# The first stage's squares added up before TensorE, wider idle products, and weight splits further ahead

## The chip, the core and the metric

The kernel runs on one core of a Trainium2 chip. A core has five engines with queues of their own: TensorE (PE in the rows; its weight loads are listed apart as PEld), VectorE (DVE), ScalarE (ACT), GpSimd (POOL) and SyncE (SP, which here issues the DMA transfers). Each engine takes its instructions in the order in which the program lists them and waits on semaphores for what it needs. The metric is the device time of one execution, in microseconds (us).

## What is computed

The reference runs two transformer blocks on 256 tokens of 1024 features in float32. Only the beginning of the first block matters here:

```python
def rms_norm(x, g):
    xf = x.astype(jnp.float32)
    y = xf * lax.rsqrt(jnp.mean(xf * xf, axis=-1, keepdims=True) + EPS)
    return (y * g.astype(jnp.float32)).astype(x.dtype)
...
silu_c, silu_cc = jax.nn.silu(c), jax.nn.silu(c_ctx)
mod_x = (silu_c @ w_ada + b_ada)[:, None, :]
mod_c = silu_cc @ w_ada + b_ada
px = modulate(rms_norm(x, g_pre_mix), sh_m, sc_m) @ w_in
pc = modulate(rms_norm(ctx, g_pre_mix), csh_m, csc_m) @ w_in
```

Here x and ctx are 256 x 1024 each and w_in projects to attention and mLSTM inputs. After that come windowed attention, a gated recurrent memory (mLSTM), an output projection and a feed-forward layer, and then a second block of the same size.

## The kernel before

**Layout.** Tokens lie along the free axis and features along the 128 partitions: x is the tile `X` (inside `XT`), ctx is `CT`, each 8 feature tiles (k = 0 to 7) of 256 tokens. Every weight product is made of three in a reduced-precision float type: `prep_item` (line 377) takes the next piece of weights from the buffer `raw`, ScalarE copies its high part to `H` (line 384), VectorE subtracts to get the low part `L` (line 385), and `mm3` (lines 430 to 432) multiplies H with the high part of x, H with the low part and L with the high part.

**The list of pieces.** A planner fixes one list of pieces in the order of use. Most are weight pieces of up to eight 128-column blocks. Between them stand 1024-wide rows of the modulation matrix ("ada" pieces below), for which `prep_item` issues one VectorE reduction (line 391) instead of a split. Raw pieces are loaded by SyncE into six buffers, a new load when a buffer is read out (line 374). `block` (line 412) hands out the next block; when it takes a new piece it first prepares pieces until `la` + 1 are ready, so `la` is how many pieces are split ahead of the one in use. There are four buffers each for H and L. The first stage uses eight weight pieces, w0 to w7, one for each k; the next ones are M0, M1, M2 (the run `mkak`, 24 blocks), V0, V1, V2 (the run `v1`, 8 blocks in pieces of 3, 3 and 2), then one piece for each step of `MIX1` (q2, o0, ...). With w2 to w5, and with each of M0 to V2, goes one ada piece behind the weight piece.

**`start`, the first stage.** The inputs are loaded, `awake` issues idle products of a tile of ones (line 629) as the loads arrive, and the squares of x and ctx are made in four halves of 4 feature tiles x 256 tokens (three by ScalarE, line 642, one by VectorE, line 640). TensorE sums them over the features: for each half 8 products with one output column (line 645). The sums go through a square root (line 693) and five small VectorE steps to a diagonal matrix (line 533). `mod_rows(k)` (line 661) computes the shift and scale of feature tile k from an `araw` tile of 1 MB, `mod_cols` and `mod_of` put them into columns. A 512-column product (line 706) spreads the roots over the partitions as `psb`. `inp(k)` makes the normalised, modulated input of tile k in high and low parts (VectorE line 683, ScalarE line 684, VectorE line 687). Then a loop over k runs `mod_rows(k + 1)` and 24 products of the tile (12 of 336 columns, 12 of 256), and in its middle prepares the next weight piece and `inp(k + 1)`.

**`mix1`.** It copies the stage's results out, rotates two query tiles (`rope`), and runs `mkak` and `v1` while `ml_gates`, `conv` and `ml_ctx` advance step by step in hooks between the blocks. All of these are on VectorE and ScalarE in the order in which the program lists them. `ml_ctx` makes `kw` on VectorE from a transposed key tile, and TensorE then multiplies it (line 983).

Of the kernel before, what the change touches and what calls it, by code (L numbers as in the profile page):

```python
# [13 lines left out]
AF = mybir.ActivationFunctionType  # L14
ALU = mybir.AluOpType
# [4 lines left out]
KD = 8  # L20
SEQ = 256
# [7 lines left out]
MIX1 = (  # L29
    "A c c c q2 c a0 A o0 a1 b0 A a2 A b1 A a3 b2 q3 b3 A t o1 A t t t t t o2 A m t A t k o3 A s"  # L30
)
WAKE = (14, 4, 4, 4, 4)
ADA0 = (0, 0, 1, 1, 1, 1, 0, 0)
ADA1 = (1, 1, 1, 1, 1, 1, 1, 1, 1, 1, 1, 1)
BACK = 8
# [279 lines left out]
class Builder:  # L315
# [112 lines left out]
    def mm3(self, out, H, L, xh, xl, start, stop):  # L428
        T = self.T
        T.matmul(out, H, xh, start=start, stop=False)  # L430
        T.matmul(out, H, xl, start=False, stop=False)  # L431
        T.matmul(out, L, xh, start=False, stop=stop)  # L432
# [144 lines left out]
    def start(self):  # L577
        A, V, G, T, S = self.A, self.V, self.G, self.T, self.S
# [8 lines left out]
        with self.tc.tile_pool(name="start", bufs=1) as p:  # L587
            CT = self.tile(p, [128, KD, SEQ], "CT")
            X = self.XT[:, :, NM:]
            parts = (slice(0, 4), slice(4, 8))  # L590
# [8 lines left out]
            def load_ada(k):  # L599
                if k < KD:  # L600
                    raws[k] = self.tile(p, [128, KD, 2 * 128], "araw", bufs=4)
                    S.dma_start(raws[k], self.d["ada"][k])
# [13 lines left out]
            cs = self.tile(p, [128, KD, 32], "cs")  # L616
            self.ones = self.tile(self.pl, [128, 128], "ones")
            V.memset(self.ones, 1.0)
            V.memset(cs, 0.0)
            self.zeros = self.tile(self.pl, [128, 16], "zeros")  # L620
            V.memset(self.zeros, 0.0)
# [2 lines left out]
            psw = self.ps("mm")  # L624

            def awake(n):

                for _ in range(n):
                    T.matmul(psw[:, 0:128], self.ones, self.ones, start=True, stop=True)

            awake(WAKE[0])
            A.activation(cs[:, :, 0], self.v("c"), AF.Silu)
            A.activation(cs[:, :, 1], self.v("cc"), AF.Silu)
            tiles = [(128 * i, 128) for i in range(4)]
            pst = self.ps("sm")
            for s, src in enumerate((X, CT)):
                for i, c in enumerate(parts):
                    sq = self.tile(p, [128, 4, SEQ], f"sq{s}{i}")
                    if (s, i) == (1, 0):
                        V.tensor_tensor(sq, src[:, c], src[:, c], op=ALU.mult)  # L640
                    else:
                        A.activation(sq, src[:, c], AF.Square)
                    for t in range(2):
                        for k in range(4):
                            T.matmul(pst[:, 2 * s + t:2 * s + t + 1], sq[:, k, 128 * t:128 * t + 128], self.ones[:, 0:1],
                                     start=s + i + t + k == 0, stop=s + i + t + k == 6)
                    awake(WAKE[1 + 2 * s + i])
            self.root_table()
            ba = self.v("b_ada")
            b1 = self.tile(p, [128, KD], "b1")  # L650
# [6 lines left out]
            def mod_rows(k):  # L657

                for j in range(KD):
                    g = 32 * (j % 4)  # L660
                    T.matmul(psr[g:g + 32, 0:256], cs[:, j, :], raws[k][:, j, :], start=j < 4, stop=j >= 4)
                rows[k] = self.tile(p, [128, 256], "row", bufs=2)
                A.activation(rows[k], psr[:, 0:256], AF.Copy)
                load_ada(k + 4)

            def mod_cols(k):

                cols[k] = self.ps("sm")
                for i in range(2):
                    T.matmul(cols[k][:, 2 * i:2 * i + 2], rows[k][:, 128 * i:128 * i + 128], self.v("sel"), start=True,  # L670
                             stop=True)

            def mod_of(k):
                ps = cols.pop(k)
                V.tensor_scalar(M[:, k, :], ps[:, 0:2], b1[:, k:k + 1], self.v("g_pre_mix")[:, k:k + 1], op0=ALU.add,
                                op1=ALU.mult)
                V.tensor_scalar(SH[:, k, :], ps[:, 2:4], ba[:, k:k + 1], None, op0=ALU.add)

            def inp(k, R):
                t = self.t2()  # L680
                for s, src in enumerate((X, CT)):
                    c = slice(SEQ * s, SEQ * s + SEQ)
                    V.scalar_tensor_tensor(t[:, c], src[:, k, :], M[:, k, s:s + 1], R[:, c], op0=ALU.mult, op1=ALU.mult)
                    A.activation(self.xh[:, k, c], t[:, c], AF.Identity, bias=SH[:, k, s:s + 1])
                for s in range(2):
                    c = slice(SEQ * s, SEQ * s + SEQ)
                    V.scalar_tensor_tensor(self.xl[:, k, c], t[:, c], SH[:, k, s:s + 1], self.xh[:, k, c].bitcast(F32),
                                           op0=ALU.add, op1=ALU.subtract)
# [3 lines left out]
            a = self.tmp([128, 16], "rs_a", F32)[:, :4]  # L692
# [5 lines left out]
            V.scalar_tensor_tensor(r, a, 1.5, r, op0=ALU.add, op1=ALU.mult)  # L698
            dg = self.diag(r, tiles)
            mod_rows(0)  # L700
            self.la = 0
            self.prep_item()
            mod_cols(0)
# [10 lines left out]
            for k in range(KD):  # L714
                if k < KD - 1:
                    mod_rows(k + 1)
                first, last = k == 0, k == KD - 1
                H, L = self.block()
                for i, ps in enumerate(main):
                    o = slice(128 * i, 128 * i + 128)  # L720
                    self.mm3(ps[:, :336], self.xh[:, k, o], self.xl[:, k, o], H, L, first, last)
                    if i == 1:
                        lows = []
                        if k < KD - 2:
                            self.prep_item(lows)
                        if k < KD - 1:
                            mod_cols(k + 1)
                            mod_of(k + 1)
                            inp(k + 1, R)
                        for f in lows:  # L730
                            f()
                        if k == 0:
                            A.activation(self.cbx, self.cbx, AF.Silu)
                        if 0 <= k < 4 or k == KD - 1:
                            self.prep_item()
                for i, out in enumerate(outs):
                    H, L = self.block()

                    self.mm3(out, H, L, self.xh[:, k, 0:SEQ], self.xl[:, k, 0:SEQ], first and i % 2 == 0, last and i % 2 == 1)
            self.la = 1  # L740
            self.held, self.heldp = main, outs

    def mods(self):
# [22 lines left out]
    def mix1(self):  # L766
        A, V, G, T = self.A, self.V, self.G, self.T
        both, xo = slice(0, 512), slice(0, SEQ)
        with self.tc.tile_pool(name="mix1", bufs=1) as p:
# [68 lines left out]
            for i, _ in enumerate(self.vproj("v1", (0, 128, 256, 384), ev)):  # L838
                if i < 3:
                    next(gates, None)  # L840
                if i == 0:
                    next(convs[1])
                if i == 3:
                    for c in (2, 3, 0, 1):
                        next(convs[c])
                if i in (5, 7):
                    next(ctxs)
                if i in (1, 4):
                    self.la += 1
            for _ in gates:  # L850
                pass
# [5 lines left out]
                A=lambda: next(att), c=lambda: next(ctxs, None), t=lambda: next(tail, None),  # L857
                k=lambda: self.ahead(-1), K=lambda: self.ahead(1), a=self.ml_a, b=self.ml_b, q=rope_q, o=gate_o, m=self.mods, s=lambda: A.activation(mo, mo, AF.Sigmoid),
# [846 lines left out]
```

## Time and profile before

| | |
|---|---|
| median of 3 executions | 1041.27 us (1039.15 to 1042.88) |
| the profiled execution | 1044.65 us, of which 1042.9 us are the span from the first to the last instruction |
| TensorE busy | 1000.4 us (96% of the span) |
| VectorE, ScalarE, GpSimd busy | 650.5, 492.6, 192.7 us |
| moved by DMA | 175.64 MB, mean 168 GB/s |
| granted TensorE clock, mean | 0.963 of 2.4 GHz |

The profile is of one execution. Busy shares are means over the whole span, so what a change in the first 120 us is worth has to be read from that stretch alone. A time in brackets behind a row is how long the engine stood still before the instruction, and what ended that.

### The profile page before, as it was taken

How to read it: one execution, taken by the hardware profiler on the slowest of the kernel's cores; microseconds unless marked ns; L12 is line 12 of the kernel's file. 1: busy time of each engine (PE TensorE's matmuls, PEld its weight loads, DVE VectorE, ACT ScalarE, POOL GpSimd, SP SyncE). 2: the span in 40 equal slices, each digit the busy share in tenths (PEclk: the TensorE clock that was granted, in tenths of full speed). 3: DMA queues.
4: the chain of work that ended last, by engine and by line, in shares of the span. 5: the costliest groups of instructions: out<-in, count | busy, mean ns of one | idle time of the engine just before them, and what ended most of it. 6: DMA issues, size and time to landing. Idle time of an engine off the chain costs nothing. (4 is left out here: it accounts for less than half of the span.)

```text
span 1042.9 us, 18997 instructions
## 1 busy us (share of the span) xinstructions
PE 1000.4 (96%) x7698; PEld 940.7 (90%) x7698; DVE 650.5 (62%) x1150; ACT 492.6 (47%) x833; POOL 192.7 (18%) x205
## 2 busy tenths in 40 slices
PE   9997999988999999889999999999988999999996
PEld 9785757788999999889999999998877999999995
DVE  1777756877788744666555454567375866566543
ACT  2545454665544444354444443644444545544441
POOL 0020002351000000421111121125463421111000
PEclk6898999989999999899999999999998999999998
DMA  9852612464568655245555555253233555555531
GB/s 364 314 175 88 228 41 81 133 232 141 196 226 270 220 183 183 93 149 182 182 167 178 166 179 177 102 169 135 83 121 113 190 183 182 187 189 191 182 122 41
DMA packets 48503, 175.64 MB, mean 168 GB/s; under 512 B 5392, under 2 KB 6688, under 8 KB 47392
## 3 DMA queue, kind: packets, MB, share of 16 engines
q1 hardware_dynamic: 48416, 174.43, 49.7%
q8 instruction: 60, 0.98, 0.4%
q14 instruction: 27, 0.22, 0.1%
HBM read 173.36 MB, written 1.05 MB: 167 GB/s over the span
## 5 line engine op out<-in xcount | busy, mean ns | idle before, releaser
L385 DVE TENSOR_TENSOR L<-raw,H 128x1024 fp32r<-128x1024 f32 (+2 forms) x259 | 319.9, 1236 | 235.8 <-ACT H L384 235.6
L384 ACT ACTIVATE H<-raw 128x1024 fp32r<-128x1024 f32 (+2 forms) x278 | 288.6, 1045 | 187.5 <-issue 82.2
L431 PE MATMUL mm<-x,H 128*128 128x256 f32 (+3 forms) x1016 | 290.7, 286 | 0.0
L430 PE MATMUL mm<-x,H 128*128 128x256 f32 (+3 forms) x984 | 284.4, 289 | 3.3 <-ACT x L1218 3.3
L432 PE MATMUL mm<-x,L 128*128 128x256 f32 (+3 forms) x984 | 281.1, 286 | 0.0
L431 PEld LDWEIGHTS mm<-x,H 128*128 128x128 f32 x1016 | 194.2, 191 | 0.9 <-DVE x L1220 0.5
L430 PEld LDWEIGHTS mm<-x,H 128*128 128x128 f32 x984 | 188.3, 191 | 6.4 <-ACT x L1218 4.2
L432 PEld LDWEIGHTS mm<-x,L 128*128 128x128 f32 x984 | 187.9, 191 | 0.4
L430 PE MATMUL at<-x,H 128*128 128x256 f32 (+3 forms) x512 | 148.9, 291 | 1.5 <-ACT H L384 1.5
L432 PE MATMUL mm<-hh,L 128*128 128x256 f32 (+1 forms) x528 | 150.3, 285 | 0.0
L430 PE MATMUL mm<-hh,H 128*128 128x256 f32 (+1 forms) x528 | 149.7, 283 | 0.0
L431 PE MATMUL mm<-hl,H 128*128 128x256 f32 (+1 forms) x528 | 149.5, 283 | 0.0
L432 PE MATMUL at<-x,L 128*128 128x256 f32 (+3 forms) x512 | 148.6, 290 | 0.5 <-DVE L L385 0.5
L431 PE MATMUL at<-x,H 128*128 128x256 f32 (+3 forms) x512 | 148.5, 290 | 0.0
L430 PEld LDWEIGHTS at<-x,H 128*128 128x128 f32 x512 | 98.3, 192 | 2.4 <-ACT H L384 1.9
L432 PEld LDWEIGHTS at<-x,L 128*128 128x128 f32 x512 | 98.2, 192 | 1.6 <-DVE L L385 1.0
L430 PEld LDWEIGHTS mm<-hh,H 128*128 128x128 f32 x528 | 99.6, 189 | 0.0
L431 PEld LDWEIGHTS mm<-hl,H 128*128 128x128 f32 x528 | 99.4, 188 | 0.0
L432 PEld LDWEIGHTS mm<-hh,L 128*128 128x128 f32 x528 | 99.3, 188 | 0.0
L431 PEld LDWEIGHTS at<-x,H 128*128 128x128 f32 x512 | 98.3, 192 | 0.6
L499 POOL TENSOR_TENSOR acc<-acc,t 128x256 f32<-128x256 f32 (+1 forms) x42 | 40.3, 960 | 238.8 <-ACT t L1175 177.6
L1275 POOL TENSOR_TENSOR g<-g,R 128x272 f32<-128x272 f32 (+1 forms) x44 | 33.3, 760 | 216.3 <-ACT g L1274 216.3
(372 smaller groups left out, 1331.9 us busy)
## 6 DMA issues: line engine op xcount, KB each, us to landing
raw<-wst SPq DMA_DIRECT2D x293, 512.0 KB, 3.3
araw<-ada SPq DMA_DIRECT2D x8, 1024.0 KB, 8.5
raw<-wst SPq DMA_DIRECT2D x8, 424.0 KB, 7.7
raw<-wst SPq DMA_DIRECT2D x6, 480.0 KB, 3.8
XT<-xin SPq DMA_DIRECT2D x2, 544.0 KB, 4.3
CT<-cin SPq DMA_DIRECT2D x2, 512.0 KB, 6.6
out<-XT SPq DMA_DIRECT2D x8, 128.0 KB, 2.0
raw<-wst SPq DMA_DIRECT2D x3, 320.0 KB, 2.8
```

Source lines behind the costliest of these rows:

```text
L384: self.A.activation(H[:, :w], src, AF.Copy)
L385: low = lambda: (self.G if self.poolsplit else self.V).tensor_tensor(L[:, :w], src, H[:, :w].bitcast(F32), op=ALU.subtract)
L430: T.matmul(out, H, xh, start=start, stop=False)
L431: T.matmul(out, H, xl, start=False, stop=False)
L432: T.matmul(out, L, xh, start=False, stop=stop)
L499: self.G.tensor_tensor(st["acc"], st["acc"], sq, op=ALU.add)
L1275: G.tensor_tensor(g, g, R[:, :n], op=ALU.mult)
```

## The change

It makes four edits. In `start`, all four squares are ScalarE's; VectorE then adds the two halves of each input (1024 columns), folds the sum once more (512 columns), and TensorE's one-column products fall from 32 to 8. The idle products take a 256-column tile of ones in place of a 128-column one; their numbers go from 14, 4, 4, 4, 4 to 14, 4, 2, and 2 more behind `mod_rows(0)`. In the loop over k, the pieces M0 and M1 with their ada pieces are prepared at k = 6 and 7 (before: M0 alone at 7). And `la` is 2 in `mkak` and rises to 3 in `v1` at once (before: 1, then 2, then 3).

```diff
--- before.py
+++ after.py
@@ -29,7 +29,7 @@
 MIX1 = (
     "A c c c q2 c a0 A o0 a1 b0 A a2 A b1 A a3 b2 q3 b3 A t o1 A t t t t t o2 A m t A t k o3 A s"
 )
-WAKE = (14, 4, 4, 4, 4)
+WAKE = (14, 4, 2, 2)
 ADA0 = (0, 0, 1, 1, 1, 1, 0, 0)
 ADA1 = (1, 1, 1, 1, 1, 1, 1, 1, 1, 1, 1, 1)
 BACK = 8
@@ -616,6 +616,8 @@
             cs = self.tile(p, [128, KD, 32], "cs")
             self.ones = self.tile(self.pl, [128, 128], "ones")
             V.memset(self.ones, 1.0)
+            awakes = self.tile(p, [128, SEQ], "awake")
+            V.memset(awakes, 1.0)
             V.memset(cs, 0.0)
             self.zeros = self.tile(self.pl, [128, 16], "zeros")
             V.memset(self.zeros, 0.0)
@@ -626,25 +628,27 @@
             def awake(n):
 
                 for _ in range(n):
-                    T.matmul(psw[:, 0:128], self.ones, self.ones, start=True, stop=True)
+                    T.matmul(psw[:, 0:SEQ], self.ones, awakes, start=True, stop=True)
 
             awake(WAKE[0])
             A.activation(cs[:, :, 0], self.v("c"), AF.Silu)
             A.activation(cs[:, :, 1], self.v("cc"), AF.Silu)
             tiles = [(128 * i, 128) for i in range(4)]
             pst = self.ps("sm")
-            for s, src in enumerate((X, CT)):
-                for i, c in enumerate(parts):
-                    sq = self.tile(p, [128, 4, SEQ], f"sq{s}{i}")
-                    if (s, i) == (1, 0):
-                        V.tensor_tensor(sq, src[:, c], src[:, c], op=ALU.mult)
-                    else:
-                        A.activation(sq, src[:, c], AF.Square)
-                    for t in range(2):
-                        for k in range(4):
-                            T.matmul(pst[:, 2 * s + t:2 * s + t + 1], sq[:, k, 128 * t:128 * t + 128], self.ones[:, 0:1],
-                                     start=s + i + t + k == 0, stop=s + i + t + k == 6)
-                    awake(WAKE[1 + 2 * s + i])
+            sq = [[self.tile(p, [128, 4, SEQ], f"sq{s}{i}") for i in range(2)] for s in range(2)]
+            A.activation(sq[0][0], X[:, parts[0]], AF.Square)
+            A.activation(sq[0][1], X[:, parts[1]], AF.Square)
+            A.activation(sq[1][0], CT[:, parts[0]], AF.Square)
+            A.activation(sq[1][1], CT[:, parts[1]], AF.Square)
+            for s in range(2):
+                a, b = sq[s]
+                V.tensor_tensor(a, a, b, op=ALU.add)
+                V.tensor_tensor(a[:, 0:2], a[:, 0:2], a[:, 2:4], op=ALU.add)
+                for t in range(2):
+                    for k in range(2):
+                        T.matmul(pst[:, 2 * s + t:2 * s + t + 1], a[:, k, 128 * t:128 * t + 128], self.ones[:, 0:1],
+                                 start=k == 0, stop=k == 1)
+                awake(WAKE[1 + s])
             self.root_table()
             ba = self.v("b_ada")
             b1 = self.tile(p, [128, KD], "b1")
@@ -698,6 +702,7 @@
             V.scalar_tensor_tensor(r, a, 1.5, r, op0=ALU.add, op1=ALU.mult)
             dg = self.diag(r, tiles)
             mod_rows(0)
+            awake(WAKE[3])
             self.la = 0
             self.prep_item()
             mod_cols(0)
@@ -721,7 +726,7 @@
                     self.mm3(ps[:, :336], self.xh[:, k, o], self.xl[:, k, o], H, L, first, last)
                     if i == 1:
                         lows = []
-                        if k < KD - 2:
+                        if k != KD - 2:
                             self.prep_item(lows)
                         if k < KD - 1:
                             mod_cols(k + 1)
@@ -731,13 +736,16 @@
                             f()
                         if k == 0:
                             A.activation(self.cbx, self.cbx, AF.Silu)
-                        if 0 <= k < 4 or k == KD - 1:
+                        if k < 4 or k == KD - 1:
+                            self.prep_item()
+                        if k == KD - 2:
+                            self.prep_item()
                             self.prep_item()
                 for i, out in enumerate(outs):
                     H, L = self.block()
 
                     self.mm3(out, H, L, self.xh[:, k, 0:SEQ], self.xl[:, k, 0:SEQ], first and i % 2 == 0, last and i % 2 == 1)
-            self.la = 1
+            self.la = 2
             self.held, self.heldp = main, outs
 
     def mods(self):
@@ -845,7 +853,7 @@
                         next(convs[c])
                 if i in (5, 7):
                     next(ctxs)
-                if i in (1, 4):
+                if i == 1:
                     self.la += 1
             for _ in gates:
                 pass
```

On TensorE, at the very start of the program, these are all the rows up to the first product of the loop. mm is a bank of PSUM for idle products, then for `psb`; sm holds the sums and the columns; sq tiles are the squares. Before:

```order
L629 MATMUL mm_116<-ones_109 128x128 x14
L645 MATMUL sm_133<-ones_109,sq_25_134 128x1 x8
L629 MATMUL mm_116<-ones_109 128x128 x4
L645 MATMUL sm_133<-ones_109,sq_26_148 128x1 x8
L629 MATMUL mm_116<-ones_109 128x128 x4
L645 MATMUL sm_133<-ones_109,sq_27_162 128x1 x8
L629 MATMUL mm_116<-ones_109 128x128 x4
L645 MATMUL sm_133<-ones_109,sq_28_176 128x1 x8
L629 MATMUL mm_116<-ones_109 128x128 x4
L661 MATMUL at_196<-araw_86,cs_108 32x256 x8
L670 MATMUL sm_229<-vec_69,row_219 128x2 x2
L706 MATMUL mm_233<-t_37_206,ones_109 128x512
```

And in the changed kernel:

```order
L631 MATMUL mm_118<-awake_111,ones_109 128x256 x14
L649 MATMUL sm_135<-ones_109,sq_26_136 128x1 x4
L631 MATMUL mm_118<-awake_111,ones_109 128x256 x4
L649 MATMUL sm_135<-ones_109,sq_28_138 128x1 x4
L631 MATMUL mm_118<-awake_111,ones_109 128x256 x2
L665 MATMUL at_168<-araw_86,cs_108 32x256 x8
L631 MATMUL mm_118<-awake_111,ones_109 128x256 x2
L674 MATMUL sm_203<-vec_69,row_191 128x2 x2
L711 MATMUL mm_207<-t_38_178,ones_109 128x512
```

Two of the four groups of one-column products are gone, the others are half as long, and two wide idle products stand behind the first `mod_rows`.

On VectorE, where the first stage ends and `mix1` begins, L is the low part of a piece, ISA with MOD the reduction of an ada piece (two instructions), gi and gz the gates. The first L below is M0's in both. Before:

```order
L385 TENSOR_TENSOR L_641<-raw_393,H_640 128x1024
L786 MEMSET t_117_682 128x512
...
L896 TENSOR_TENSOR t_124_708<-at_252,cst_70 128x256
L391 ISA raw_409,MOD_73<-raw_409,cbx_72 128x1024
L391 ISA MOD_73 128x1
L385 TENSOR_TENSOR L_718<-raw_448,H_717 128x1024
L803 TENSOR_SCALAR gi_672<-sm_730,vec_69 64x512
L919 TENSOR_SCALAR gz_673<-gz_673,vec_69 64x512
L391 ISA raw_464,MOD_73<-raw_464,cbx_72 128x1024
L391 ISA MOD_73 128x1
L385 TENSOR_TENSOR L_771<-raw_503,H_770 128x1024
```

And in the changed kernel:

```order
L385 TENSOR_TENSOR L_591<-raw_367,H_590 128x1024
L391 ISA raw_383,MOD_73<-raw_383,cbx_72 128x1024
L385 TENSOR_TENSOR L_624<-raw_422,H_623 128x1024
L391 ISA raw_438,MOD_73<-raw_438,cbx_72 128x1024
L794 MEMSET t_123_668 128x512
...
L904 TENSOR_TENSOR t_130_694<-at_226,cst_70 128x256
L385 TENSOR_TENSOR L_701<-raw_477,H_700 128x1024
L811 TENSOR_SCALAR gi_658<-sm_713,vec_69 64x512
L927 TENSOR_SCALAR gz_659<-gz_659,vec_69 64x512
L391 ISA raw_529,MOD_73<-raw_529,cbx_72 128x1024
L385 TENSOR_TENSOR L_754<-raw_594,H_753 128x960
```

Ahead of the gates now stand the splits of M0, M1 and M2 and two ada reductions, where M0, M1 and one reduction stood; behind gz comes V0's split in place of M2's.

## Rows read from the trace of the kernel before

**Rows 1.** Busy us of each engine by stretch; granted clock, DMA share, GB/s.

```profile
10.00:26.00 16.00, 16.00 (x87) 15.06 (x86) 1.61 (x9) 2.38 (x4) 0.00 (x0) 0.51 1.01 420
95.00:100.00 5.00, 5.00 (x23) 4.87 (x21) 3.72 (x9) 1.42 (x4) 0.00 (x0) 0.59 0.51 175
...
100.00:120.00 20.00, 18.17 (x124) 15.54 (x123) 19.30 (x32) 10.23 (x19) 2.33 (x2) 0.91 0.69 255
```

**Rows 2.** Timeline, 7 to 25 us: start, length, engine, line, instruction, count.

```profile
7.06 1.84 PE L645 MATMUL sm<-ones,sq 128*128 128x1 f32 x16
8.30 1.23 DVE L640 TENSOR_TENSOR sq<-CT 128x1024 f32<-128x1024 f32 x1 [7.00 <-DMA CT<-cin]
8.77 1.14 PE L629 MATMUL mm<-ones 128*128 128x128 f32 x8
9.57 1.06 ACT L642 ACTIVATE sq<-CT 128x1024 f32<-128x1024 f32 x1 [2.08 <-DMA CT<-cin]
16.73 0.33 SPq L615 DMA_DIRECT2D cst<-cst  x1
19.43 3.41 PE L645 MATMUL sm<-ones,sq 128*128 128x1 f32 x16
22.88 0.26 ACT L693 ACTIVATE rs_y<-sm,eps 128x4 f32<-128x4 f32 x1 [10.74 <-PE sm L645]
24.05 0.87 DVE L533 TENSOR_SCALAR t<-cst,rs_y 128x128 f32<-128x128 f32 x4
24.69 1.94 PE L661 MATMUL at<-araw,cs 128*32 128x256 f32 x16
```

**Rows 3.** Timeline, 28 to 63 us.

```profile
28.00 2.05 PE L706 MATMUL mm<-t,ones 128*128 128x512 f32 x2
31.85 0.65 PE L430 MATMUL mm<-H,x 128*128 128x336 f32 x1
36.86 1.07 PE L661 MATMUL at<-araw,cs 128*32 128x256 f32 x16
37.86 0.42 PE L430 MATMUL mm<-H,x 128*128 128x336 f32 x1
43.43 0.91 ACT L384 ACTIVATE H<-raw 128x848 fp32r<-128x848 f32 x1
45.36 0.91 ACT L684 ACTIVATE x<-t,SH 128x256 fp32r<-128x256 f32 x2 [1.02 <-DVE t L683]
62.73 0.42 PE L430 MATMUL mm<-H,x 128*128 128x336 f32 x1
```

**Rows 4.** DMA issues of 0 to 140 us: count, KB each, us to landing.

```profile
araw<-ada SPq DMA_DIRECT2D x8, 1024.0 KB, 8.5
raw<-wst SPq DMA_DIRECT2D x8, 424.0 KB, 7.7
```

**Rows 5.** DMA issues of 16 to 18 us, the same columns.

```profile
raw<-wst SPq DMA_DIRECT2D x1, 512.0 KB, 13.1
cst<-cst SPq DMA_DIRECT2D x1, 392.0 KB, 13.0
```

**Rows 6.** Timeline of VectorE, 72 to 117 us.

```profile
72.59 1.76 DVE L385 TENSOR_TENSOR L<-raw,H 128x1024 fp32r<-128x1024 f32 x1
76.73 1.20 DVE L391 CUSTOM_DVE_ANT_0 raw<-raw,cbx 128x1024 f32<-128x1024 f32 x1
82.96 1.23 DVE L385 TENSOR_TENSOR L<-raw,H 128x1024 fp32r<-128x1024 f32 x1 [5.03 <-ACT H L384]
115.92 1.28 DVE L973 TENSOR_TENSOR kw<-at,CO 128x512 f32<-128x512 f32 x2
```

**Rows 7.** TensorE's waits, 0 to 140 us: total us, times, longest.

```profile
PE mm L431 <- DVE L L385: 5.5, 2, 4.7
PE at L430 <- ACT H L384: 1.5, 1, 1.5
```

**Rows 8.** Timeline of TensorE, 105 to 200 us.

```profile
116.66 3.38 PE L983 MATMUL at<-bl,kw 128*64 128x129 f32 x32
```

## Prediction

> **What bounds the kernel now.** The page's first part has TensorE busy for 96% of the span, so whatever shortens the time must come from where TensorE waits or runs slowly. I read the busy times by stretch first, because they show the granted clock: between 10 and 26 us TensorE counts as fully busy, but at a mean clock of 0.51, that is at the lower of its two levels, 1.2 GHz [rows 1]. The timeline says with what: one-column products of the squares and 128-column idle products. Sixteen records of the one-column kind took 1.84 us before the clock fell and 3.41 us after [rows 2]. The last of them end at 22.84 us, and ScalarE's square root had waited 10.74 us for that. ScalarE's last square was done at 9.57 + 1.06 = 10.63 us. So for twelve microseconds the beginning hangs on TensorE doing almost no work, slowly. The first useful product starts at 31.85 us [rows 3]. That is the stall the change aims at first.
>
> The second place is the mixing stage's beginning, 82 to 104 us. The list of waits has TensorE waiting 5.5 us for low parts of weights and 1.5 us for a high part [rows 7], and a half clock follows the longest wait: 0.59 over 95 to 100 us [rows 1]. VectorE is the busy one there. Its own long gap is 5.03 us ahead of M2's split, ended by ScalarE's H [rows 6], which is queued behind the gates' logarithm.
>
> **The start, step by step.** The last square still ends at 10.63 us: ScalarE now does the third square too, from 8.30 us, when VectorE's could begin because the data were there, and at the 1.06 us of its other squares it is done before the fourth begins at 9.57 [rows 2]. VectorE's add of 1024 columns is priced by its multiplication of the same size, 1.23 us; the 512-column fold by one of the two 512-column products of `kw`, 0.64 us [rows 2, 6]. So the sum of ctx is there at 10.63 + 0.05 + 1.23 + 0.64 = 12.55 us. Ahead of its one-column products TensorE has 14 wide idle products, x's products and 4 more idle ones. I let those end by 12.6 us; they can end half a microsecond later if the clock rises late at the start, and I keep that for the range. Four one-column products are 8 records: 8 x 1.84 / 16 = 0.92 us at the full clock, 8 x 3.41 / 16 = 1.71 at half [rows 2]. Full: done at 13.5 us against 22.84.
>
> From there two chains run side by side. The root takes 24.05 + 0.87 - 22.84 = 2.08 us, to 15.6 [rows 2]. TensorE goes through 2 wide idle products, `mod_rows(0)`, 2 more, the two column products, `psb`. Four 128-column idle products took 1.14 us, so two of twice the width are 1.14 too; `mod_rows` is 1.07 us at full clock and 1.94 at half; `psb` is 2.05 at half, so 1.03 at full [rows 2, 3]; for the columns I take 0.5 us, about four of the slow one-column records with a wait for the row. Sum: 13.5 + 1.14 + 1.07 + 1.14 + 0.5 + 1.03 = 18.4 us. Neither chain waits for the other: the root is early by then. From the end of `psb` (30.05) to the first product (31.85) it takes 1.80 us now, on VectorE and ScalarE [rows 3]. First product: 20.2 us, **11.65 us earlier**.
>
> The first feature tile costs 37.86 - 31.85 = 6.01 us, later ones (62.73 - 37.86) / 5 = 4.97 [rows 3]; the difference, **1.0 us**, is the half clock still there, and goes if the clock is up.
>
> **Does the data arrive?** Starting the loop earlier presses on the transfers, which now hide. All loads up to the constants are issued by 16.73 us and the last lands at 29.7 [rows 2, 5], whatever TensorE does; the 16 DMA engines are saturated at 420 GB/s meanwhile [rows 1]. Behind them come, in SyncE's order, araw 4, w4, an ada piece, araw 5, w5, ada, araw 6, w6, w7, araw 7. By their sizes (1024, 424, 512 KB [rows 4, 5]) an araw takes 2.5 us, a w piece 1.03, an ada piece 1.25. So w4, w5, w6 land at 33.2, 38.0 and 42.8 us. ScalarE queues each piece's H ahead of the next tile's x, and each takes 0.91 us [rows 3]; x of tiles 3, 4, 5 is then ready at 35.0, 39.8 and 44.6. TensorE wants them at 20.2 + 1.0 x 4.97 per tile: 35.1, 40.1, 45.1. It fits, with nothing to spare, and the shift lasts through the loop. I take **0.6 us** off for what is late.
>
> The trace moved 420 GB/s [rows 1]. The Trainium skill (DMA: Bandwidth & Descriptors, Where 436 GB/s comes from) says the HBM side binds such transfers at about 358 GB/s per core. The trace disagrees with it here, so the sum goes by 420. By 358 the 5.5 MB from araw 4 to w6 would take 15.4 us in place of 13.1, and the saving would be an estimated 2.3 us smaller.
>
> **The mixing stage.** M2's pieces are now split before the gates' logarithm, so the 1.5 us wait goes, and V0's L comes at the place in VectorE's order where M2's was, ahead of use. But VectorE works in order, and total work does not fall. Ahead of the gates it now has M0, ada, M1, ada, M2 where it had M0, ada, M1: one ada (1.20) and one split (1.2 to 1.76) more [rows 6], less about 1.2 us in which it idled there. The gates, hence the 5.03 us gap behind ScalarE, come 1 to 2 us later; after it, one ada and one split fewer remain (2.4 us) up to `kw`. So V1 and V2 wait for their L instead (I expect some 3 us each), and what really counts is `kw` at 115.92, which releases TensorE's line 983 at 116.66 [rows 6, 8]; after that TensorE runs on. `kw` gains 2.4 - 1.5 = **0.9 us**. From both sides: a loss of 0.6 if the gates' delay is the whole extra work of 1.20 + 1.76 = 2.96; a gain of 9 us if VectorE does not bind and all waits and the half clock go (7.0 [rows 7] and 2.1 of the slow clock).
>
> **Sum.** 11.65 + 1.0 - 0.6 + 0.9 = 12.95 us. The profiled execution took 1044.65 us, so its like would be 1031.7; it was 3.4 us over the median, and I take the saving from the median: 1041.27 - 12.95 = **1028.3 us**. A measurement can tell about 0.3%, 3.1 us, from no change.
>
> **The rivals.**
> *The clock falls again near the start.* It fell at about 10.3 us (a mean of 0.51 over 10 to 26 us [rows 1]); what ran before were one-column products with one group of narrow idle ones between; the edit gives more width, but also pauses and `mod_rows` with 32 columns of weights. If it is down from the second one-column group to the first tile, the chain is 12.6 + 1.71 + 2.28 + 1.94 + 2.28 + 1.0 + 2.05 + 1.80 = 25.7, a gain of 6.2 and none of the 1.0: total saving 6.2 + 0.9 = 7.1 us, now without the transfers' loss: 1034.2 us. If it falls only for the last stretch before the first tile, 1 to 2 us are lost: that is within my forecast's range. The Trainium skill (TensorE: Matmul & The Clock Gate, What's actually happening) says the slow clock is the default and activity releases it. By that rule the wide products keep it up only if they count as enough; the trace agrees as far as half clock followed idle time at 95 us. Chance 0.22.
> *The waits in the mixing stage really go.* Then 9 us in place of 0.9: 1020.2 us. For it: every wait in the list names H or L. Against it: VectorE is busy for 19.30 of the 20 us from 100 to 120 [rows 1]. Chance 0.13.
> *Transfers bind the loop (a slower kernel).* Place: w7, whose H stands ahead of tile 6's x, and so of the product now at 62.73 us; to be no later than now it must land by 62.73 - 2 x 0.91 = 60.9 us [rows 3]. From 29.7 us on, 5.9 MB stand up to it (three araw, four w pieces, two ada pieces [rows 4, 5]), so below 190 GB/s the early start is worth nothing; at 170 w7 is 3.7 us late, and the time 1041.27 + 3.7 - 0.9 = 1044.1. For it: SyncE issues in order, and a load that waits for its buffer holds all behind it. Against it: 420 GB/s as long as loads are queued. A milder form (370 GB/s) costs 1 to 2 us and lies within the range. Chance 0.02 for slower, 0.04 for a loss that ends within 0.3%.
> *The change does nothing to the start*, because the one-column products were not what the root waited for: excluded by ScalarE's 10.74 us wait on line 645 [rows 2].
>
> **How the numbers follow.** Forecast 0.58, with 1025.5 to 1031.5 as its own range (a late first rise of the clock, 0 to 2 us from transfers, 0 to 3 us gained or lost in the mixing). Clock rival 0.22 (1032 to 1036), mixing rival 0.13 (1018 to 1025), transfers and the rest 0.07. Leaving a part of each tail, the range is 1022.5 to 1035. Faster by over 0.3% means below 1038.1: 0.94; within 0.3%: 0.04; slower: 0.02.
>
> **What would show it.** In the changed profile: the square root at 13.5 to 14.5 us; a clock of 0.9 or more from 14 to 30 us; the first 336-column product near 20; tiles of 5.0 us; no ScalarE wait on a load over 1 us between 30 and 45; M2 without a wait, V1 and V2 with waits for L, and line 983 about 13.5 us earlier than 116.66. The forecast is wrong if the clock is at half at 18 us, if the tiles are longer than 5.3 us, or if V1 and V2 start without waiting.

## The result, and the profile after

The changed kernel took 1025.77 us (median of 4 executions, 1024.61 to 1031.98) beside 1041.65 us for the kernel before (1039.15 to 1042.88). The ratio is 0.9863, with a 95% interval of 0.9819 to 0.9906, which lies below 1: faster, 15.9 us by these medians. The forecast was 1028.3 us in a range of 1022.5 to 1035.0. The profiled execution took 1025.65 us, 1023.8 of them span, against 1044.65.

The start first. Busy time by stretch of the changed kernel; the columns are TensorE, its weight loads, VectorE, ScalarE, GpSimd, then the granted clock, the DMA share and GB/s:

```profile
10.00:26.00 16.00, 14.97 (x117) 10.69 (x116) 10.58 (x27) 9.49 (x16) 0.00 (x0) 1.00 1.01 420
...
80.00:90.00 10.00, 1.23 (x8) 0.68 (x6) 8.77 (x20) 2.59 (x5) 0.00 (x0) 0.77 0.32 105
```

Between 10 and 26 us the clock is at its upper level, 1.00 against 0.51 [rows 1]. The timeline of TensorE, whose line numbers are up to 8 higher now:

```profile
10.19 0.95 PE L649 MATMUL sm<-ones,sq 128*128 128x1 f32 x8
...
13.12 1.05 PE L649 MATMUL sm<-ones,sq 128*128 128x1 f32 x8 [0.15 <-DVE sq L646]
...
15.07 1.07 PE L665 MATMUL at<-araw,cs 128*32 128x256 f32 x16
...
17.41 1.11 PE L711 MATMUL mm<-t,ones 128*128 128x512 f32 x2
...
19.84 0.42 PE L430 MATMUL mm<-H,x 128*128 128x336 f32 x1 [0.33 <-ACT x L688]
...
21.79 0.61 PE L674 MATMUL sm<-vec,row 128*128 128x2 f32 x4 [0.55 <-ACT row L667]
...
25.78 0.42 PE L430 MATMUL mm<-H,x 128*128 128x336 f32 x1
...
27.33 0.61 PE L674 MATMUL sm<-vec,row 128*128 128x2 f32 x4 [0.35 <-ACT row L667]
```

The first useful product starts at 19.84 us in place of 31.85 [rows 3], 12.01 earlier. The second tile starts at 25.78 (37.86 before, 12.08 earlier), the third at 31.34, 11.6 earlier (before it stood at 42.95). How much earlier an instruction comes than its counterpart in the profile of before is called the shift from here on. ScalarE's timeline shows what it has ahead of the rows that TensorE waits for, and its waits for loads:

```profile
14.21 0.26 ACT L697 ACTIVATE rs_y<-sm,eps 128x4 f32<-128x4 f32 x1 [1.62 <-PE sm L649]
...
24.66 1.28 ACT L738 ACT_TABLE_LOAD   x1
25.95 1.06 ACT L738 ACTIVATE cbx<-cbx 128x1024 f32<-128x1024 f32 x1
26.91 0.36 ACT L667 ACTIVATE row<-at 128x256 f32<-128x256 f32 x1
...
33.48 0.91 ACT L384 ACTIVATE H<-raw 128x848 fp32r<-128x848 f32 x1 [1.56 <-DMA raw<-wst]
...
38.65 0.91 ACT L384 ACTIVATE H<-raw 128x848 fp32r<-128x848 f32 x1 [1.78 <-DMA raw<-wst]
```

TensorE's waits of 0 to 140 us (line and what it waited for, total us, times, longest):

```profile
PE sm L964 <- ACT gz L954: 4.7, 1, 4.7
PE sm L964 <- ACT gz L948: 2.7, 1, 2.7
PE sm L964 <- issue: 1.4, 1, 1.4
...
PE sm L674 <- ACT row L667: 0.9, 2, 0.5
```

The waits for L and H [rows 7] are gone. In their place 8.8 us stand at line 964, the transposes of the gates, and TensorE is busy for only 1.23 of the 10 us from 80 to 90. VectorE's timeline answers to [rows 6], and TensorE's to [rows 8]:

```profile
73.65 1.16 DVE L385 TENSOR_TENSOR L<-raw,H 128x960 fp32r<-128x960 f32 x1 [4.96 <-ACT H L384]
...
103.90 1.28 DVE L981 TENSOR_TENSOR kw<-at,CO 128x512 f32<-128x512 f32 x2
```

```profile
106.43 1.98 PE L991 MATMUL at<-bl,kw 128*64 128x129 f32 x32
```

VectorE's gap behind ScalarE is as long as before (4.96 against 5.03 us), only ahead of another split. `kw` comes 12.02 us earlier, but line 991 only 10.23 (106.43 against 116.66): it starts 2.5 us behind `kw` now, so it no longer waits for it. Before, its products ran at half clock (3.38 us for what takes 1.98 now). From 118 us on in the kernel before, up to 779, the two traces keep a distance of 10.9 to 13.1 us (11.6 at 125, 12.4 at 776). Then it grows to 18.6 by 797 us, far behind the last changed line. The four executions of the changed kernel lie apart by about as much as this step (three from 1024.61 to 1025.89, one at 1031.98), so it has to be understood before any median is.

**The place near 780 us.** In the second block, near 782 us before and 769 us now, VectorE multiplies two 1024-column tiles (line 1555 before, 1563 now; in the rows AT and F), and GpSimd makes four weight splits (line 385). In what follows this is called the meeting. VectorE's row, then GpSimd's, of the kernel before:

```profile
781.98 3.37 DVE L1555 TENSOR_TENSOR AT<-AT,F 128x1024 f32<-128x1024 f32 x1
```

```profile
774.76 9.51 POOL L385 TENSOR_TENSOR L<-raw,H 128x1024 fp32r<-128x1024 f32 x4 [5.82 <-ACT H L384]
```

And of the changed kernel:

```profile
769.49 1.21 DVE L1563 TENSOR_TENSOR AT<-AT,F 128x1024 f32<-128x1024 f32 x1
```

```profile
762.31 7.11 POOL L385 TENSOR_TENSOR L<-raw,H 128x1024 fp32r<-128x1024 f32 x3 [5.81 <-ACT H L384]
769.60 3.33 POOL L385 TENSOR_TENSOR L<-raw,H 128x1024 fp32r<-128x1024 f32 x1 [0.19 <-ACT H L384]
```

In these rows whichever starts first finishes, and the other is held. Before, GpSimd's four splits end at 784.27, and the product at 785.35, 1.08 us behind them. In the changed kernel the product starts 0.11 us ahead of the fourth split, which then takes 3.33 us in place of 7.11 / 3 = 2.37. The Trainium skill (SBUF — State Buffer, Who interferes with whom) says that a VectorE instruction with two SBUF inputs and a GpSimd instruction that reads SBUF exclude each other, and that the order of issue decides who is blocked; both traces agree, 3.37 and 1.21 us for the same product. What the 2.2 us cost follows in the kernel before: TensorE waits 3.43 us at line 1596 for a successor of the product, and its clock is at half behind that wait:

```profile
786.00 0.69 PE L1596 MATMUL at<-cst,t 128*128 128x128 f32 x2 [3.43 <-DVE t L1563]
```

```profile
785.00:796.00 11.00, 10.00 (x38) 6.22 (x39) 5.14 (x12) 2.75 (x6) 2.83 (x4) 0.53 0.15 49
```

In the changed kernel the stretch at the same distance behind the product's start, 12.5 us earlier, reads:

```profile
772.50:783.50 11.00, 11.00 (x86) 9.49 (x85) 5.32 (x11) 7.53 (x11) 3.99 (x6) 1.00 0.40 124
```

### The profile page after: what moved, and what is told of

Read it like the earlier page. It is cut to its first block, busy times and chain, and to the rows that moved or that the text cites. A ratio compares the mean times of both kernels' runs of the same rounds, so it can differ in the third digit from the quotient of the medians.

```text
span 1023.8 us, 18874 instructions
## 1 busy us (share of the span) xinstructions
PE 981.8 (96%) x7634; PEld 924.2 (90%) x7634; DVE 649.2 (63%) x1154; ACT 493.8 (48%) x834; POOL 191.5 (19%) x205
## 6 DMA issues: line engine op xcount, KB each, us to landing
araw<-ada SPq DMA_DIRECT2D x8, 1024.0 KB, 13.0
```

## Experiments

**1 and 2. Either half of the change alone.** First the edits to the start, with the pieces M0 to V2 prepared as before:

```diff
-                        if k != KD - 2:
+                        if k < KD - 2:
...
-            self.la = 2
+            self.la = 1
...
-                if i == 1:
+                if i in (1, 4):
                     self.la += 1
```

> The start's edits alone, the mixing stage as before. Theory A (the whole gain is the earlier start; the mixing edits give nothing, because VectorE's order up to kw binds that stage): first 336-column product at 20 us, line 983's products 10 to 12 us earlier than before, time 1025 to 1029 us, within 0.2% of the changed kernel. Theory B (the mixing edits carry several of the 16 us): 3 to 6 us slower than the changed kernel, 1029 to 1033 us, line 983's products only 6 to 8 us earlier than before.

Measured: 1032.22 us (12 executions, 1025.52 to 1034.98), ratio 0.9923 [0.9893, 0.9953]. The first product starts at 19.46 us and the shift is 12.6 us at 125 us and 12.9 at the end. The weights' waits are those of before, 4.5 us for L and 1.2 for H. The time lies in theory B's range, while `kw`'s products, 11.4 us earlier than before, lie in A's. The times alone cannot decide between the two, because they hold two groups here too: two executions up to 1027.75 and ten from 1030.91 on. In this trace the clock was at half for part of 22 to 26 us, about the first tile:

```profile
22.00:26.00 4.00, 4.00 (x23) 3.86 (x26) 2.92 (x8) 2.98 (x4) 0.00 (x0) 0.57 1.02 425
```

Then the mixing's edits with the start of before (the start's part of the diff undone):

> The mixing edits alone, the start as before. Theory A: 1040 to 1043 us, no change that can be told; line 983's products within 1.5 us of 116.66; the waits for low parts of weights are gone and come back as waits of the gates' transposes. Theory B: 1035 to 1038 us, line 983's products 4 to 6 us earlier.

Measured: 1037.41 us (12 executions, 1030.62 to 1044.45), ratio 0.998 [0.9944, 1.0016]: no difference that can be told. Its trace has the three waits at the gates' transposes again:

```profile
PE sm L959 <- ACT gz L949: 4.5, 1, 4.5
PE sm L959 <- ACT gz L943: 2.7, 1, 2.7
PE sm L959 <- issue: 1.5, 1, 1.5
```

So these waits come with the splits further ahead, not with the earlier start, and they take back what the removed ones gave. The median lies in theory B's range, but 3.1 us of this trace's shift stand at its first product already, which came at 28.78 us: the clock was at 0.57 over 10 to 26 us and 0.73 over 24 to 34, against 0.51 and 0.50 in the profile of before. The shift is 4.9 us at 125 us. Run 12, without these edits, gains as much on the way there (3.8 us at 60 us, 5.5 at 125), so the growth is not the edits'.

**3 and 4. Who holds the gates back?** Two `conv` steps stood in hooks 9 and 13 of `mkak`, behind V0's split on VectorE; they are moved to hook 7, ahead of it:

```diff
-            for i, c in ((9, 2), (13, 3), (17, 0)):
-                hooks[i] = lambda c=c: next(convs[c])
+            hooks[7] = lambda: (next(convs[2]), next(convs[3]))
+            hooks[17] = lambda: next(convs[0])
```

> The changed kernel with two convolution steps (2.6 us of VectorE work) moved ahead of V0's split, into VectorE's 5 us gap behind ScalarE's logarithm. Theory A (VectorE's order binds the stage): the waits of the gates' transposes shrink by 2 to 2.6 us, line 983's products (991 here) at 104 us in place of 106.4, time 2 to 2.6 us below the changed kernel. Rival (ScalarE's chain binds, whatever VectorE does): no change, 106.4 us.

Measured: 1027.02 us (6 executions, 1022.48 to 1030.86), ratio 0.9882 [0.9836, 0.9928]. Line 991 comes at 103.11 us, 3.3 earlier than in the changed kernel, and 14.9 us of shift stand at 125 us instead of 11.6. The mean of the six, 1026.79 us, is 2.1 us under that of the changed kernel's ten in run 5 (1028.85). The waits of TensorE between 60 and 140 us:

```profile
PE sm L964 <- ACT gz L954: 4.6, 1, 4.6
PE sm L964 <- ACT gz L948: 1.6, 1, 1.6
```

Next the six reductions behind M0 to V2 were replaced by copies of one column (those six columns of the modulation are then not the reference's):

> The changed kernel without six of the 1.21 us reductions of the modulation (those behind M0 to V2): each is a copy of one column, so the modulation is not the reference's. Theory A: the gates' transposes come 3 to 4 us earlier and line 983's products (991 here) 5 to 6 us earlier, at 100 to 101.5 us. Rival (ScalarE or TensorE binds): less than 1.5 us earlier.

Measured: 1022.11 us in one execution, whose trace is of the lower group (the product near 766 us, which is explained above, took 1.21 us); line 991's counterpart comes at 102.89 us, 3.5 us earlier, and the waits at the transposes are 3.4, 2.7 and 0.6 us. Less than was expected, but of the same kind: in both runs the VectorE work taken from ahead of the gates shortens TensorE's wait for them. Even so 6.2 us of it stay in run 3 and 6.7 in run 4, and no run takes these apart.

**5. The changed kernel once more.**

> The changed kernel once more, for more executions. If its times fall into two groups some 7 us apart (about 1025 and about 1032 us), as the four first did, the median says which group is commoner; the theory that the whole gain is the 11.6 us of the start (and the rest is which group an execution falls in) expects a mean gain of 10 to 13 us over the kernel before. The rival (a steady gain of 16 us) expects nearly all executions at 1024 to 1026.

Measured: 1031.76 us (6 executions, 1025.85 to 1032.84) beside 1040.29 (23 executions, 1032.34 to 1046.57), ratio 0.9895 [0.9863, 0.9927]. With the first four there are ten executions of the changed kernel: five from 1024.61 to 1025.89 and five from 1031.63 to 1032.84, none between. The two medians, 1025.77 and 1031.76, differ by how many of each fell into the sample. The mean of run 5 lies 10.8 us under that of before beside it (1030.07 and 1040.89), within the 10 to 13 us that were expected.

**6. Splits near 770 us away from GpSimd, first try.** The last two of GpSimd's splits were given to VectorE, but the switch was turned back behind them, and the following splits, which VectorE makes in the changed kernel, went to GpSimd:

```diff
         V.tensor_tensor(flat(sg), flat(sg), flat(self.F[:, 0:4]), op=ALU.mult)
+        self.poolsplit = False
...
                 yield
+                self.poolsplit = POOL2
```

> The changed kernel with two weight splits at about 770 us moved from GpSimd to VectorE, so that none runs on GpSimd beside the 1024-column product of the gate (line 1563). Theory (the two groups are executions in which this product takes 3.4 us beside GpSimd's split, TensorE then waits and its clock falls, and executions in which it takes 1.2 us): line 1563 takes 1.2 us in the profile, no wait of 3.4 us on line 1571 (line 1572 here), and no group at 1030 to 1033 is left; 1022 to 1027 us throughout. Rival (the groups come from elsewhere): two groups as before.

Measured: 1040.14 us (12 executions, 1036.59 to 1041.95). The shift is 18.8 us at 797 us, 8.9 at 851 and 5.1 at the end: what was gained was lost again in the splits that had moved to GpSimd, 2.4 us each against 1.2 on VectorE. The time is far from the 1022 to 1027 us that were expected. The product took 1.21 us here and no two groups appear, but with so much else changed this doesn't settle the theory.

**7 and 8. The start taken apart.** The adds with the idle products of 128 columns (`ones` in place of `awakes`):

> The changed kernel with the idle products 128 columns wide again, their numbers (14, 4, 2, 2) unchanged. Theory C (the wide idle products matter through the clock): the clock is at half somewhere between 10 and 20 us, the first 336-column product comes at 22 to 25 us, 2 to 5 us later than in the changed kernel. Rival D (the additions on VectorE and the fewer one-column products do it all): the first product at 19 to 20.5 us, the clock full.

Measured: 1027.71 us (4 executions, 1026.47 to 1034.49), ratio 0.9885 [0.9848, 0.9923]. Stretch and timeline:

```profile
10.00:22.00 12.00, 12.00 (x58) 9.01 (x62) 5.06 (x16) 3.59 (x6) 0.00 (x0) 0.50 1.02 422
```

```profile
9.95 1.87 PE L649 MATMUL sm<-ones,sq 128*128 128x1 f32 x8 [3.06 <-DVE sq L646]
...
13.52 1.71 PE L649 MATMUL sm<-ones,sq 128*128 128x1 f32 x8
...
23.50 0.42 PE L430 MATMUL mm<-H,x 128*128 128x336 f32 x1
```

The clock is at half from 10 us on, each step of the chain is slow, and the first product starts at 23.50, 3.7 us later than in the changed kernel. But the narrow products also end sooner, and TensorE stood idle for 3.06 us ahead of the first sums, so this run doesn't tell width from idle time. The next one does. Now the kernel before with nothing but the wide idle products:

> The kernel before with the idle products 256 columns wide, the 32 one-column products and the numbers (14, 4, 4, 4, 4) unchanged. Theory C: the clock stays full and the one-column groups take 1.84 us each, but four of them with the idle products between end at 22 to 24 us, so the square root is no earlier; the rest runs at full clock and the first 336-column product comes at 28 to 30 us, 2 to 4 us earlier than before. Rival E (the clock alone is the gain): the first product at 22 us or earlier.

Measured: 1039.39 us (10 executions, 1032.12 to 1042.92), ratio 0.9969 [0.9942, 0.9995].

```profile
10.00:26.00 16.00, 15.50 (x115) 13.71 (x113) 1.61 (x9) 2.97 (x6) 0.00 (x0) 1.00 1.02 421
```

```profile
20.72 1.84 PE L647 MATMUL sm<-ones,sq 128*128 128x1 f32 x16
...
29.10 0.42 PE L430 MATMUL mm<-H,x 128*128 128x336 f32 x1 [0.62 <-ACT x L686]
```

TensorE is busy for 15.5 of these 16 us, and for all of them in the kernel before, where the clock was at 0.51 [rows 1]; only the width differs, and the clock is full. But the last sums still end at 22.56 us (22.84 before), and the first product gains 2.75 us on the profile of before. The adds with the shorter list of idle products gain 8.35 (31.85 to 23.50), both together 12.0. This is what theory C of both runs says: the sums are the larger part, and the width counts once the list is short. The gains are smaller against two other traces that begin as the kernel before does, runs 2 and 12, whose first products came at 28.78 and 28.07 us: against these the wide products alone gain nothing, and the adds alone 4.6 to 5.3 us.

**9 and 10. The two splits, mended; and both gains together.** As in 6, without the second line, so that the splits behind stay on VectorE:

> The changed kernel with the last two of the splits that GpSimd makes near 765 to 775 us given to VectorE, and nothing else; the splits behind them stay with VectorE, as they are in the changed kernel. Theory (the two groups of times, some 7 us apart, come from the 1024-column product of line 1563 meeting these splits: 3.37 us against 1.21, and a wait of TensorE behind it): all executions fall in one group, between 1022 and 1028 us, the median some 3 us under the changed kernel's; the product takes 1.2 to 1.3 us in the profile, and the shift against the kernel before is 17 us or more from 797 us to the end. Rival (the clock alone makes the groups, and the product is only its companion): two groups as before, about 1025 and 1032.

Measured: 1025.82 us (6 executions, 1025.43 to 1027.60), ratio 0.9871 [0.9823, 0.9919]: one group, as the theory expects. The product in its trace:

```profile
767.74 1.21 DVE L1563 TENSOR_TENSOR AT<-AT,F 128x1024 f32<-128x1024 f32 x1
```

With the `conv` steps moved as in 3:

> The changed kernel with the two splits near 770 us on VectorE and the two conv steps of the mixing ahead of V0's split. If both gains add (3.3 us at 103 us of which 3 stay, and the faster group always): median 1019 to 1024 us, one group, ratio to before about 0.981. Rival (the gain in the mixing is given back on the way, or the groups remain): 1024 to 1031, as the runs with the conv steps alone.

Measured: 1024.22 us (6 executions, 1023.50 to 1025.03), ratio 0.9852 [0.9809, 0.9896]. In 3 the same kernel without the moved splits had three executions at 1022.5 to 1024.0 and three at 1030.1 to 1030.9; here all six lie within 1.5 us. The theory of the meeting holds, and the version is steadier than the changed kernel, 4.6 us under the mean of its ten executions (1028.85). By the means it gains 1.9 us against 9, of the 3 that the trace shows at 125 us, so its median lies just above the range for gains that add (1019 to 1024).

**11 and 12. The size of the change without the groups.** The start's edits alone, with the two splits moved:

> The change's edits to the start alone, the weight splits of the mixing two and three items ahead as before, and the last two of GpSimd's splits near 770 us given to VectorE, as in the run of the changed kernel with these two splits moved (1025.4 to 1027.6 us). With the two groups of times gone, the difference of the two tells what the splits further ahead are worth. Theory (nothing: the waits only move from the weights to the gates' transposes): 1024 to 1027 us. Rival (the splits ahead do pay, by the forecast's 0.9 us or more): 1027 to 1030 us; or by the 7 us of waits that they remove: above 1031.

Measured: 1027.99 us (6 executions, 1025.44 to 1030.37), ratio 0.9884 [0.985, 0.9917]. The median lies in the range of the rival, that the splits ahead do pay. Beside 9 the mean is 1.9 us higher, with a 95% interval of 0.0 to 3.7 worked out from the two spreads, and on another chip. The traces do not put it into the mixing: the shift at 125 us is 11.5 us here and 11.6 in 9. They part between 230 and 690 us, to 10.5 here and 12.1 in 9 at 776 us, and they do so where the clock of one is at half and that of the other is not: 0.79 here and 1.00 in 9 over 232 to 240 us, 0.94 and 1.00 over 640 to 670. Run 1, with the same edits as 11 up to there, stands at 12.3. So the traces show the spread of executions rather than the edits, but whether the edits pay some microseconds on the mean is left open.

This trace also shows the meeting undone: GpSimd has two splits there, and the product is short.

```profile
769.34 1.21 DVE L1560 TENSOR_TENSOR AT<-AT,F 128x1024 f32<-128x1024 f32 x1
```

> The kernel before with the same two splits given to VectorE and nothing else. With the two groups gone, its distance to the changed kernel with the two splits moved (1025.8 us) is what the change is worth without the chance of the groups. Theory (the groups come from the meeting near 780 us, in the kernel before too; the change is worth the 11.6 us of its shift): the spread shrinks, the median is 1036 to 1039, and no run is above 1041. Rival (the kernel before has another cause for its spread): runs still from 1031 to 1046, median about 1041.

Measured: 1035.74 us (12 executions, 1032.82 to 1039.00), ratio to before 0.9971 [0.9941, 1.0001]. No execution is above 1041 any more, while 5 of the 17 of before beside it were; a spread of 6 us stays. One cause of it is seen in three traces: the clock at the start, 0.96 over 24 to 34 us here, 0.73 in run 2 and 0.50 in the profile of before, and the first product came at 28.07, 28.78 and 31.85 us. The program up to there is the same. Without the meeting near 780 us, the change is worth 1035.74 - 1025.82 = 9.9 us (9.8 by the means, with a 95% interval of 8.2 to 11.4 worked out from the two spreads; the two ran on different chips).

## Why the prediction was right, and where not

**The start** (11.65 us forecast) measured 12.01. The chain went as put down: the root at 14.21 us (13.5 to 14.5 named), `mod_rows` and `psb` at full clock, the columns 0.50 us (four of the slow one-column records, by which the forecast explained its 0.5, would be 0.85). The sum of ctx was half a microsecond late (ScalarE's last square at 10.02, behind its load), and the stretch from `psb` to the first product shorter, 1.3 us instead of 1.80. The rival that the clock falls again did not come about in this trace; run 7 shows that it would have, had the idle products stayed narrow, and in run 1, with the same start, the clock was at 0.57 over 22 to 26 us, a mild form of it. But the saving is measured from an execution of before in which the clock was at half from about 10 us into the first tile. Two others of that start began their first product 3.1 and 3.8 us sooner, which fits the 9.9 us, rather than 12, that are left between the kernels when both have the two splits moved. So the term is right for the profiled execution and some 2 to 4 us too large against these others: the forecast took one trace for the kernel.

**The first tile** (1.0 us) failed: 5.94 us against 6.01. The step said that its extra length was the half clock and would go with it. The clock is full now, but a new wait has taken its place, which the step put at nothing: the tile waits 0.55 us for ScalarE's row copy, which stands behind two x, R and an H in ScalarE's queue. In the second tile it is the table load and the silu of `cbx`, 2.3 us ahead of the row: 0.35 us of wait, and the tile takes 5.56 us.

**The transfers** (-0.6 us): the size fits by chance, the place doesn't. The shift fell by 0.5 us in the loop, in the second tile just named. ScalarE waited 1.5 to 1.8 us for weights, more than the 1 us that was given as a limit, and TensorE lost nothing by it: its list has no wait in the loop but those two. The transfers ran at 418 to 420 GB/s, so by no more than in the kernel before. The Trainium skill (DMA: Bandwidth & Descriptors, Where 436 GB/s comes from) would have the HBM bind at about 358; the trace again shows more.

**The mixing** (+0.9 us) measured nothing: the shift is 11.6 us at the third tile and 11.6 at 125 us. The step that failed is where the wait goes. I followed VectorE's order and put the new wait at the L of V1 and V2. But the gates' transposes stand in hooks in TensorE's own queue, behind V0's second block, and they wait for the gates, which the extra split and reduction hold back by 3.0 us (`gi` comes 8.6 us earlier where the stage comes 11.6; 1 to 2 us were forecast). So TensorE stops there, inside V0 and ahead of V1 and V2. VectorE's order then gives back what it took, as forecast, and the low parts of V1 and V2 were ready. Runs 2 to 4 show the place, and that VectorE's order ahead of the gates sets a part of the wait. Nor was `kw` what counts: line 991 came 10.2 us earlier, not 13.5, and TensorE, held up at the gates, was the later one. The rival that the waits really go was wrong for the same reason.

**The sum** was 12.95 us, and at 125 us the profiled traces differ by 11.6: 12.0 + 0.1 - 0.5 + 0.0. They stand at 12.4 at 776 us. Most of the rest of the 19 us between them at the end is the meeting near 780 us, which the forecast did not know: the profile of before was an execution in which GpSimd was first, that of after one in which VectorE was. That the measured median lies only 2.5 us from 1028.3 is in part luck: three of the four executions were of the lower group. Run 5's median of 1031.76 us lies 3.5 us on the other side. The range held both groups. Of the forecast's own signs of being wrong two came: the first two tiles took 5.94 and 5.56 us, more than 5.3, and V1 and V2 started without waiting.

What tips it goes with the clock in the traces, though no run sets the clock on purpose. In run 1 ScalarE made the fourth H at 767.13 us, and GpSimd went on without a gap and held the product; in the changed kernel ScalarE made that H at 768.46, and VectorE was first by 0.11 us. The clock ahead of the product was at full in run 1 and not in the changed kernel. Run 1's rows, over 640 to 670 us, ahead of the product and the product itself:

```profile
640.00:670.00 30.00, 29.40 (x194) 28.32 (x193) 16.70 (x30) 17.94 (x28) 3.92 (x3) 0.94 0.36 113
762.00:770.00 8.00, 6.14 (x52) 6.14 (x53) 6.40 (x7) 3.67 (x6) 7.53 (x4) 1.00 0.38 133
769.67 3.36 DVE L1560 TENSOR_TENSOR AT<-AT,F 128x1024 f32<-128x1024 f32 x1
```

The first two of the changed kernel:

```profile
640.00:670.00 30.00, 28.96 (x200) 27.63 (x199) 16.60 (x32) 17.80 (x28) 3.90 (x3) 1.00 0.33 109
761.00:769.00 8.00, 5.30 (x32) 5.30 (x33) 5.56 (x6) 3.99 (x7) 6.69 (x3) 0.79 0.32 101
```

All nine traces with the splits in their places are of one of these two kinds. In before and runs 1 to 3 the clock is 0.94 over 640 to 670 us and 1.00 in the 8 us ahead of the product, the product takes 3.36 to 3.37 us, and TensorE waits 3.4 us behind it. In the changed kernel and runs 4, 5, 7 and 8 it is 1.00 over 640 to 670 and 0.79 ahead of the product, the product takes 1.21 us, and that wait is not there. Run 11, with the splits moved, has the clock of the first kind, and its product takes 1.21 us all the same: its GpSimd splits ended at 768.99 us, ahead of the product, so it is the meeting that makes the product long. Why an execution is of one kind or the other stays open. The small steps between 230 and 690 us stand at such stretches too: the distance to before goes from 11.6 to 13.1 us where the clock of before is at 0.79 (244 to 252 us) and that of the changed kernel at 1.00 over the same work (232 to 240).

## What to carry to other kernels

A wait that is removed by preparing something earlier can come back wherever the same queue now delivers later; look for every consumer of that queue, and in the waiting engine's own queue for what stands ahead of the work that was to gain. Where a kernel's times fall into two groups, line up a trace of each and look for the place where the distance jumps, before a saving is read from medians or from one pair of traces. At a start that waits for a long chain with little work, take the number of steps down first, then look at the granted clock there, and if idle products leave it at half, try wider ones.

## What the runs showed of the hardware

A 1024-column product of VectorE takes 1.21 us, or 3.36 to 3.37 when GpSimd's split began before it; GpSimd's split takes 2.4 us, or 3.33 when the product was first. Who starts first, by 0.11 us in the one execution, is worth some 6 us of a 1026 us kernel (12.4 to 18.6 us of distance): where GpSimd was first, a wait of 3.4 us and a clock of 0.53 over 785 to 796 us followed.

With idle products of 128 columns between one-column products the clock was at 0.51 over 10 to 26 us in the kernel before, although TensorE was busy throughout; with 256 columns at the same places it was at 1.00 (run 8). Sixteen records of the one-column kind took 1.84 us at full clock and 3.41 us at half.
